# A hybrid attention and state-space block: the last two gate quarters as one pass behind the state-space part

## The chip, the cores and the metric

The kernel runs on one core of a Trainium2 chip. The time is device microseconds for one execution, measured on three runs: 1385.44, 1385.53 and 1386.13 us, median 1385.53. Besides, one execution was recorded by the hardware profiler; its span, from the first to the last instruction, is 1383.8 us, with a mean granted TensorE clock of 0.998.

Names of engines: PE is TensorE (PEld its weight loads), DVE is VectorE, ACT is ScalarE, POOL is GpSimd, SP is SyncE, which here only issues DMAs.

## The reference

256 tokens of width 2048 are normalised and multiplied with one wide matrix `w_in`, whose columns are split into the inputs of an attention branch (q, k, v and a gate z_a), of a state-space branch (z_s, xs, B, C, dt) and two branch gates (g_a, g_s):

```python
hn = rms_norm(x, norm_w)
proj = hn @ w_in
q, k, v, z_a, z_s, xbc, dt_raw, g_a, g_s = jnp.split(proj, split_points, axis=-1)
# attention: 16 heads of 128, three dilated windows, mixed by their log-sum-exp; times silu(z_a)
# state space: causal convolution of 4 taps and silu on xbc, then a chunked scan in 8 groups;
#   y + d_skip * xs, times silu(z_s), rms_norm over 4096
# merge: sigmoid gates g_a, g_s on (o_a @ w_attn_branch) and (y @ w_ssm_branch)
# output: merged @ w_out, plus x, final norm
```

All data is float32. The state-space part has 64 heads of 64 in 8 groups, the chunk is 128 tokens. The quantity that the change is about is g_s, the gate of the state-space branch: four quarters of 512 columns, each x (256 by 2048) times a 2048 by 512 slice of `w_in`, followed by a tanh.

## The kernel before

**Products in parts.** Each float32 operand is split into a high part and a remainder: `unit` loads 128 by 1024 weights (512 KB) through the SP queue into a ring of five, ACT copies the high part h (L276), DVE subtracts it for the remainder l (L277); h and l have four buffers each. A product is then three matmuls, xh·h, xh·l and xl·h (gemm_b L412 to L414; `triple` L476 to L478). Projections of the state-space part and of the heads use pairs, one matmul of 512 columns (L329) and one of 256 (L332).

**Order of the work.** A first block and dt come first, then quarters 0 and 1 of g_s, then the 8 groups of the state-space part. A group projects B, C, four tiles xs and four zs; some steps run later, in the middle of the next group's projections: `turn` transposes xs (tile xtp, L801), `decays` prepares the decay factors gt on ACT (L777 to L791), `scan` multiplies (tile yp, L820), and `gather` (L833 to L838, with the split at L284 and L288) makes from yp, on DVE and ACT, the gated result yT that the branch product reads. Quarter 2 of g_s stands ahead of group 4, quarter 3 behind group 7, each by `gates`. Then come passes over 1024 columns at once, by `gemm_pair`: the state-space branch (ssm, two passes of 16 quads), v (two of 8), later the 16 heads, the gate g_a, the attention branch and the output.

**Quads.** `gemm_pair` takes two k-tiles, two row halves and two column halves of 512 as a quad. A plain quad is 8 products, 24 matmuls. For the quads listed in `S_QUADS` it uses seven products, 21 matmuls (the scheme of Strassen): these need sums and differences of the weights, split into tiles ha/la, hc/lc, htt/ltt and htu/ltu (L543 on ACT, L544 on DVE; L557 makes the difference in wa), and sums of the left operand, the left factors sx_*. A left factor of x or y is computed once (`keep_left`), kept in DRAM and loaded again by `fetch_left`. The differences of the weights can be computed ahead too: `sum_jobs` loads the pieces, does two subtractions on DVE (L252, L253) and spills the result to DRAM, to be loaded as wt when its quad comes. The htt and htu tiles lie in the pool `mul`, which is opened when the pool `ssm` of the state-space part closes, and takes its memory.

**What sets the order.** Python code traces instructions; steps that are due later are put into a list by `after(ticks, f)`, where a tick is one projection or one quad. A scheduler with a timeline model and priorities then fixes each engine's own instruction order. `high_priority` lets the splits of a unit move ahead. On each engine instructions start in that order; between engines, semaphores hold an instruction until what it reads, or the memory it overwrites, is free. `behind_unit(n, f)` runs f when unit n is traced; the small POOL copy at the start of `fetch` and `fetch_left` writes one element of the destination and so holds the load on SP until that unit's h is there.

Of the kernel before, what the change touches and what calls it, by code (L numbers as in the profile page):

```python
# [38 lines left out]
GS_BEFORE = {0: (0, 1), 4: (2,)}  # L39
# [8 lines left out]
    ("ssm", 0): (5, 7, 8, 10, 11, 12, 13), ("ssm", 2): (3, 5, 7, 8, 10, 11, 12, 13),  # L48
    ("v", 0): (2, 3, 4, 5, 6), ("v", 2): (2, 4, 5, 6), ("ga", 0): (2, 4, 5, 6), ("ga", 2): (2, 4, 5, 6),
# [12 lines left out]
SUMS_SSM = [(t, q) for t in (("ssm", 0), ("ssm", 2), ("v", 0), ("v", 2)) for q in S_QUADS[t] if (t[1], q) not in IN_PLACE.get(t[0], ())]  # L62
SUM_UNITS = 2, 9, 16
# [18 lines left out]
def weight_plan():  # L82
# [22 lines left out]
    rows(("gs", 3), "w_in", OFF_GS + 3 * 512, KT)  # L105
# [91 lines left out]
def hybrid_block(ctx: ExitStack, tc: tile.TileContext, wall, xt, x, pk_d, cst_d, fw_d, out):  # L197
# [33 lines left out]

    def behind_unit(n, f):
        on_unit.setdefault(n, []).append(f)
# [4 lines left out]
    def spill(kept, key, name, src, shape):  # L238
        kept[key] = dram.tile([P, *shape], F32, name=name, tag=name)
        nc.sync.dma_start(kept[key], src)  # L240

    def sum_jobs(jobs, units, places):

        def get(tag, q, t, b11, behind):
            n = FIRST[tag] + 2 * q
            for dst, src in ((t, wall[n + 1]), (b11, wall[n, :, :512])):
                gp.tensor_copy(dst[:, 0:1], behind)
                nc.sync.dma_start(dst, src)

        def add(tag, q, t, b11, res, behind):  # L250
            gp.tensor_copy(res[:, 0:1], behind)
            ve.tensor_tensor(res[:, :512], t[:, :512], b11, ALU.subtract)  # L252
            ve.tensor_tensor(res[:, 512:], t[:, 512:], res[:, :512], ALU.subtract)  # L253
            spill(presum, (tag, q), f"t_{tag[0]}{tag[1]}_{q}", res, [UNIT])

        for n, ((tag, q), u) in enumerate(zip(jobs, units)):
            t, b11, res = places[n % len(places)]
            behind_unit(u, lambda behind, a=(tag, q, t, b11): get(*a, behind))
            behind_unit(u + SUM_LAG, lambda behind, a=(tag, q, t, b11, res): add(*a, behind))
# [7 lines left out]
    def unit(n, shape):  # L267
        if n not in loaded:
            load(n)
        w = loaded.pop(n)  # L270
        h = stream.tile([P, UNIT], F32R, name=f"h{n}", tag="h", bufs=H_BUFS)
        l = stream.tile([P, UNIT], F32R, name=f"l{n}", tag="l", bufs=H_BUFS)
        cuts = (0, UNIT // 2, UNIT) if n < N_FINE else (0, UNIT)
        with tc.high_priority(L_AHEAD) if n >= KT // UB else nullcontext():
            for a, b in zip(cuts, cuts[1:]):
                ac.activation(h[:, a:b], w[:, a:b], AF.Copy)  # L276
                ve.tensor_tensor(l[:, a:b], w[:, a:b], h[:, a:b].bitcast(F32), ALU.subtract)  # L277
# [151 lines left out]
    def fetch_left(kept, pool, bufs, key, x, spare, u):  # L429
        def get(behind):  # L430
            sx = new_sx(pool, bufs, spare, f"{key[0]}{key[1]}")
            gp.tensor_copy(sx[:, 0, 0, 0:1], behind)
            nc.sync.dma_start(sx.bitcast(F32), lefts[key])
            kept[key[1]] = left_parts(sx, x, spare)

        behind_unit(u, get)
# [248 lines left out]
    with tc.tile_pool(name="ssm", bufs=2) as sp:  # L685
# [205 lines left out]
        for c in GS_BEFORE[0]:  # L891
# [3 lines left out]
        at = sums_at[:, 3]  # L895
# [3 lines left out]
            [(sums_at[:, 0], sums_at[:, 2, :512], sums_at[:, 1])],  # L899
        )  # L900

        def left_x(q, behind):
            gp.tensor_copy(at[:, 0:1], behind)
            keep_left(("x", q), two_kts(XT, q), 0, at)
# [4 lines left out]
        for g in range(GROUPS):  # L909
# [9 lines left out]
            for t in range(max(4 * g, 1), 4 * g + 4):  # L919
                u, i = divmod(t, 2)  # L920
                acc = project(("xs", t))
                if i == 0:
                    state["xs"].append(new_pair(u, "xs"))
                if t % 4 == 3:
# [3 lines left out]
                    y_lag = Y_LAG + gate  # L928
                    for k in range(4):
# [17 lines left out]
        gates(("gs", 3), th_s, XT)  # L947
# [5 lines left out]
    def scale_gate():  # L953
        tot = bank("m1", 2, "tot_y")
# [21 lines left out]

    with tc.tile_pool(name="xp", bufs=1) as xp:
# [36 lines left out]
    behind_unit(FIRST[("v", 2)] + 1, lambda behind: fetch(dc, cst_d[:, :768], behind))  # L1014
    room = room_of(big.tile([P, 6 * 512], F32, name="room_v", tag="yo0a"), 2, 2)
    with tc.tile_pool(name="vx", bufs=1) as vx:
# [6 lines left out]
        for c in (0, 2):  # L1023
            es, prods = gemm_pair(
                ("v", c), lambda kt: XT[:, kt, :], KT, sx_of_x, c == 2, order=V_ORDERS[c], room=room
# [7 lines left out]
    with tc.tile_pool(name="att", bufs=2) as ap:  # L1033
# [33 lines left out]
        def mix(h, pT, za):  # L1067
# [10 lines left out]
            if h % 2 == 1 and q in ATT_QUADS:  # L1078
# [4 lines left out]
            [  # L1083
                (th_a[:, i, :UNIT], th_a[:, 1, UNIT + 512 * i : UNIT + 512 * i + 512], th_a[:, 0, UNIT:])
                for i in range(2)
            ],
        )

        for h in range(NH):
            q, k = (ap.tile([P, S], F32, name=f"{n}T{h}", tag=f"{n}T", bufs=2) for n in "qk")  # L1090

            for n, d in (("q", q), ("k", k)):
                evac(project((n, h)), d, f"{n}{h}")
# [22 lines left out]
    with tc.tile_pool(name="fin", bufs=2) as fp:  # L1116
# [36 lines left out]
        for n in range(4):  # L1153
# [3 lines left out]
                lambda behind, i=i, cs=cs: fetch(fin[:, i, cs], x[i * P : (i + 1) * P, cs], behind, nc.scalar),  # L1157
# [3 lines left out]
        for n, (tag, u) in enumerate(FW_BEHIND):  # L1161
            cs = slice(n * UNIT, (n + 1) * UNIT)
            behind_unit(
                FIRST[tag] + u, lambda behind, cs=cs: fetch(fw[:, cs], fw_d[cs].partition_broadcast(P), behind, nc.scalar)
# [107 lines left out]
```

## Time and profile before

| | |
|---|---|
| median of three runs | 1385.53 us |
| the profiled execution: span | 1383.8 us |
| PE busy | 1373.6 us, 99% |
| DVE busy | 1169.5 us, 85% |
| ACT busy | 835.5 us, 60% |
| POOL busy | 142.0 us, 10% |
| moved by DMA | 345.00 MB, 249 GB/s on the mean |

Busy times are sums over the whole span. The chain that ended last follows the work back from the last instruction: at each step to what released it, or to the instruction before it on its engine. A row of a group reads: line, engine, operation, out<-in, partitions by elements and type, number, then busy time and mean ns of one, then the idle time of the engine just before and what ended it. A row of the timeline begins with the start in us from the span's start and the duration, and in brackets stands the idle time before it with its releaser. PEq, ACTq, SPq are the sequencers that issue DMAs. A row of PE's waits has the total, the number and the longest. The start of scan 7 is at 580.83 us, the first matmul of the state-space branch at 583.58.

### The profile page before, as it was taken

How to read it: one execution, taken by the hardware profiler on the slowest of the kernel's cores; microseconds unless marked ns; L12 is line 12 of the kernel's file. 1: busy time of each engine (PE TensorE's matmuls, PEld its weight loads, DVE VectorE, ACT ScalarE, POOL GpSimd, SP SyncE). 2: the span in 40 equal slices, each digit the busy share in tenths (PEclk: the TensorE clock that was granted, in tenths of full speed). 3: DMA queues.
4: the chain of work that ended last, by engine and by line, in shares of the span. 5: the costliest groups of instructions: out<-in, count | busy, mean ns of one | idle time of the engine just before them, and what ended most of it. 6: DMA issues, size and time to landing. Idle time of an engine off the chain costs nothing.

```text
span 1383.8 us, 20696 instructions
## 1 busy us (share of the span) xinstructions
PE 1373.6 (99%) x7266; PEld 1169.9 (85%) x7266; DVE 1169.5 (85%) x1753; ACT 835.5 (60%) x1306; POOL 142.0 (10%) x226
## 2 busy tenths in 40 slices
PE   9999999999999999999999999999999999999997
PEld 8888888888888888888888888888888888888886
DVE  7898999987799898789889897777877788888897
ACT  7656677675667675766565554544544556655564
POOL 2301111101011100010001001111111000000112
PEclk9999999999999999999999999999999999999999
DMA  9767988868787866668677668888888757865773
GB/s 347 231 187 225 313 254 291 279 224 287 245 266 240 294 212 208 188 224 280 230 259 267 222 209 278 275 275 273 299 288 301 241 161 264 294 222 180 243 273 122
DMA packets 105080, 345.00 MB, mean 249 GB/s; under 512 B 11728, under 2 KB 13712, under 8 KB 104976
## 3 DMA queue, kind: packets, MB, share of 16 engines
q1 hardware_dynamic: 103536, 339.62, 74.0%
q10 hardware_dynamic: 1440, 4.06, 0.8%
q8 instruction: 57, 0.93, 0.3%
q14 instruction: 47, 0.39, 0.1%
HBM read 314.87 MB, written 28.77 MB: 248 GB/s over the span
## 4 chain that ended last, share of the span: by engine, by line
PE 97%; DMA 1%; DVE 1%; ACT 1%; issue 0%; SPq 0%; POOL 0%; POOLq 0%; DVEq 0%; ACTq 0%
PE ps_zs L329 8%; PE ps_xs L329 8%; PE ps_zs L332 4%; PE ps_q L329 4%; PE ps_za L329 4%; PE ps_k L329 4%; PE ps_xs L332 4%; PE ps_ssm L476 3%; PE ps_ssm L477 3%; PE ps_ssm L478 3%; PE ps_q L332 2%; PE ps_k L332 2%; PE ps_za L332 2%; PE ps_gs L414 2%; PE ps_gs L412 2%; PE ps_gs L413 2%
## 5 line engine op out<-in xcount | busy, mean ns | idle before, releaser
L276 ACT ACTIVATE h<-w 128x1024 fp32r<-128x1024 f32 (+1 forms) x398 | 413.9, 1047 | 318.0 <-issue 78.8
L277 DVE TENSOR_TENSOR l<-w,h 128x1024 fp32r<-128x1024 f32 (+1 forms) x398 | 479.4, 1211 | 124.2 <-ACT h L276 121.8
L329 PE MATMUL ps_zs<-XT,h 128*128 128x512 f32 x496 | 176.3, 397 | 0.0
L329 PE MATMUL ps_xs<-XT,h 128*128 128x512 f32 x496 | 175.9, 396 | 0.0
L332 PE MATMUL ps_zs<-XT,l 128*128 128x256 f32 x496 | 139.9, 282 | 0.0
L332 PE MATMUL ps_xs<-XT,l 128*128 128x256 f32 x496 | 139.8, 282 | 0.0
L329 PEld LDWEIGHTS ps_xs<-XT,h 128*128 128x128 f32 x496 | 93.3, 188 | 21.7
L329 PEld LDWEIGHTS ps_zs<-XT,h 128*128 128x128 f32 x496 | 93.4, 188 | 21.2
L332 PEld LDWEIGHTS ps_zs<-XT,l 128*128 128x128 f32 x496 | 93.7, 189 | 1.5 <-issue 0.7
L332 PEld LDWEIGHTS ps_xs<-XT,l 128*128 128x128 f32 x496 | 93.7, 189 | 0.4
L329 PE MATMUL ps_q<-XT,h 128*128 128x512 f32 x256 | 92.5, 405 | 0.2 <-ACT h L276 0.2
L329 PE MATMUL ps_k<-XT,h 128*128 128x512 f32 x256 | 89.9, 395 | 0.0
L329 PE MATMUL ps_za<-XT,h 128*128 128x512 f32 x256 | 89.7, 394 | 0.0
L543 ACT ACTIVATE ha<-wa 128x1024 fp32r<-128x1024 f32 x43 | 45.4, 1055 | 46.4 <-DMA wa<-in_wall 10.9
L332 PE MATMUL ps_q<-XT,l 128*128 128x256 f32 x256 | 71.2, 278 | 0.0
L332 PE MATMUL ps_k<-XT,l 128*128 128x256 f32 x256 | 71.1, 278 | 0.0
L332 PE MATMUL ps_za<-XT,l 128*128 128x256 f32 x256 | 71.1, 278 | 0.0
L544 DVE TENSOR_TENSOR la<-wa,ha 128x1024 fp32r<-128x1024 f32 x43 | 52.5, 1220 | 11.9 <-ACT ha L543 11.8
L782 ACT ACTIVATE gt<-acb,acT 128x128 f32<-128x128 f32 x128 | 44.2, 391 | 23.7 <-DMA acb<-acum_d 21.9
L329 PEld LDWEIGHTS ps_q<-XT,h 128*128 128x128 f32 x256 | 48.2, 188 | 11.5 <-ACT h L276 0.6
L329 PEld LDWEIGHTS ps_za<-XT,h 128*128 128x128 f32 x256 | 48.1, 188 | 11.3
L329 PEld LDWEIGHTS ps_k<-XT,h 128*128 128x128 f32 x256 | 48.1, 188 | 11.2
(688 smaller groups left out, 3325.1 us busy)
## 6 DMA issues: line engine op xcount, KB each, us to landing
w<-in_wall SPq DMA_DIRECT2D x394, 512.0 KB, 4.7
wa<-in_wall SPq DMA_DIRECT2D x43, 512.0 KB, 4.9
th_a<-in_wall SPq DMA_DIRECT2D x19, 512.0 KB, 5.6
sums_at<-in_wall SPq DMA_DIRECT2D x18, 512.0 KB, 4.7
acb<-acum_d SPq DMA_DIRECT2D x32, 256.0 KB, 4.0
t_ssm<-sums_at SPq DMA_DIRECT2D x13, 512.0 KB, 4.1
wt<-t_ssm SPq DMA_DIRECT2D x13, 512.0 KB, 5.4
th_a<-in_wall SPq DMA_DIRECT2D x19, 256.0 KB, 6.0
```

The lines of the kernel that those rows point to most:

```text
L276: ac.activation(h[:, a:b], w[:, a:b], AF.Copy)
L277: ve.tensor_tensor(l[:, a:b], w[:, a:b], h[:, a:b].bitcast(F32), ALU.subtract)
L329: pe.matmul(acc, h[:, kk, :], m, start=(kt == 0), stop=False)
L332: pe.matmul(acc[:, S:], l[:, kk, :], m[:, :S], start=False, stop=(kt == KT - 1))
L412: pe.matmul(accs[i], xh, h[:, kk], start=(kt == 0), stop=False)
L413: pe.matmul(accs[i], xh, l[:, kk], start=False, stop=False)
L476: pe.matmul(acc, xh, h, start=start, stop=False)
L477: pe.matmul(acc, xh, l, start=False, stop=False)
L478: pe.matmul(acc, xl, h, start=False, stop=stop)
L543: ac.activation(h, src, AF.Copy)
L544: ve.tensor_tensor(l, src, h.bitcast(F32), ALU.subtract)
L782: ac.activation(g4[:, n, b], acb[:, j, b // 2 * P : b // 2 * P + P], AF.Relu, scale=-1.0, bias=sc[:, h : h + 1],)
```

## The change

Quarters 2 and 3 of g_s become one pass of `gemm_pair`, traced behind the state-space part and ahead of the branch passes: eight quads, of which quads 4, 5 and 6 have seven products. Their three left factors are those of x that exist already for v; they are loaded into a pool `gx` at units 5, 6 and 7 of the pass. Their three presums join those made in the state-space part, 24 instead of 18, four in a group, now in place in two pairs of tiles. The decays of the last group are due 1 to 4 ticks after its next-to-last xs tile, and the lag of the scan of group 6 is 7 ticks instead of 11.

The side loads (pieces for presums, left factors, the constants dc, x and the final weights) go from the SP queue, or from ACT behind a POOL copy, to the ACT queue by `side`, whose `issue_after` places the issue behind the latest h split in ACT's order, without a POOL copy. Spills go from SP to POOL's queue. The banks of products and of direct sums are exchanged between the two passes of ssm and of v, and a few small tiles take other banks.

```diff
-GS_BEFORE = {0: (0, 1), 4: (2,)}
+GS_BEFORE = {0: (0, 1)}
+SX_G = (4, 5, 6)
+G_BEHIND = 5, 6, 7
+END_LAG = 7
...
+    ("gs", 2): SX_G,
...
-SUMS_SSM = [(t, q) for t in (("ssm", 0), ("ssm", 2), ("v", 0), ("v", 2)) for q in S_QUADS[t] if (t[1], q) not in IN_PLACE.get(t[0], ())]
-SUM_UNITS = 2, 9, 16
+SUMS_SSM = [(t, q) for t in (("gs", 2), ("ssm", 0), ("ssm", 2), ("v", 0), ("v", 2)) for q in S_QUADS[t] if (t[1], q) not in IN_PLACE.get(t[0], ())]
+SUM_UNITS = 1, 6, 11, 16
...
-    rows(("gs", 3), "w_in", OFF_GS + 3 * 512, KT)
+    pair(("gs", 2), "w_in", OFF_GS + 2 * 512, KT)
...
+    def side(dst, src, queue=nc.scalar):
+        with tc.issue_after(here["high"]):
+            queue.dma_start(dst, src)
...
-        nc.sync.dma_start(kept[key], src)
+        gp.dma_start(kept[key], src)
...
-        def add(tag, q, t, b11, res, behind):
-            gp.tensor_copy(res[:, 0:1], behind)
-            ve.tensor_tensor(res[:, :512], t[:, :512], b11, ALU.subtract)
-            ve.tensor_tensor(res[:, 512:], t[:, 512:], res[:, :512], ALU.subtract)
-            spill(presum, (tag, q), f"t_{tag[0]}{tag[1]}_{q}", res, [UNIT])
+        def add(tag, q, t, b11):
+            with tc.issue_after(here["low"]):
+                ve.tensor_tensor(t[:, :512], t[:, :512], b11, ALU.subtract)
+                ve.tensor_tensor(t[:, 512:], t[:, 512:], t[:, :512], ALU.subtract)
+            spill(presum, (tag, q), f"t_{tag[0]}{tag[1]}_{q}", t, [UNIT])
...
             sx = new_sx(pool, bufs, spare, f"{key[0]}{key[1]}")
-            gp.tensor_copy(sx[:, 0, 0, 0:1], behind)
-            nc.sync.dma_start(sx.bitcast(F32), lefts[key])
+            side(sx.bitcast(F32), lefts[key])
...
+                if t == 4 * GROUPS - 2:
+                    for k in range(4):
+                        after(1 + k, lambda a=(g, k, cb, state): decays(*a))
...
-                    y_lag = Y_LAG + gate
-                    for k in range(4):
+                    y_lag = (END_LAG if g == GROUPS - 2 else Y_LAG) + gate
+                    for k in range(4 if g < GROUPS - 1 else 0):
...
-        gates(("gs", 3), th_s, XT)
         tick(final=True)
...
+    with tc.tile_pool(name="gx", bufs=1) as gx:
+        sx_of_g = {}
+        for n, q in enumerate(SX_G):
+            fetch_left(sx_of_g, gx, len(SX_G), ("x", q), two_kts(XT, q), 0, FIRST[("gs", 2)] + G_BEHIND[n])
+        es, prods = gemm_pair(("gs", 2), lambda kt: XT[:, kt, :], KT, sx_of_g, False)
+        dst = blocks(th_s, 2)
+        fold(prods, dst)
+        for d, e in zip(dst, es):
+            ve.tensor_tensor(d, e, d, ALU.add)
+            ac.activation(d, d, AF.Tanh, scale=0.5)
...
-                ("ssm", c), lambda kt: kt_of(yT, kt), 2 * KT, sxs, c == 2, {} if c else {2: [scale_gate], **{u: [lambda q=q: left_y(q)] for q, u in Y_LATE.items()}},
+                ("ssm", c), lambda kt: kt_of(yT, kt), 2 * KT, sxs, c == 0, {} if c else {2: [scale_gate], **{u: [lambda q=q: left_y(q)] for q, u in Y_LATE.items()}},
```

Scan 7 on PE, before: it stands behind all 96 matmuls of quarter 3 (ps_gs3), directly ahead of the state-space branch (ps_ssm0).

```order
L413 MATMUL ps_gs3_1_6195<-l192_6365,XT_76 128x512
L414 MATMUL ps_gs3_1_6195<-h192_6364,XT_76 128x512
L820 MATMUL yp7_1_6393<-gt7_6196,xdt7_6241 64x256 x2
L820 MATMUL yp7_1_6393<-gt7_6196,xdt7_6241 64x128 x2
...
L820 MATMUL yp7_0_6392<-gt7_6196,xdt7_6241 64x256 x2
L820 MATMUL yp7_0_6392<-gt7_6196,xdt7_6241 64x128 x2
...
L476 MATMUL ps_ssm0_0_6441<-h193_6447,yTa_81 128x512
```

And now: it stands in the gate pass (ps_gs2), behind 73 of its matmuls.

```order
L486 MATMUL ps_gs2_3_6124<-h182_6205,XT_76 128x512
L484 MATMUL ps_gs2_0_6121<-h183_6237,XT_76 128x512
L828 MATMUL yp7_1_6074<-gt7_5860,xdt7_6060 64x256 x2
L828 MATMUL yp7_1_6074<-gt7_5860,xdt7_6060 64x128 x2
...
L828 MATMUL yp7_0_6073<-gt7_5860,xdt7_6060 64x256 x2
L828 MATMUL yp7_0_6073<-gt7_5860,xdt7_6060 64x128 x2
...
L485 MATMUL ps_gs2_0_6121<-l183_6238,XT_76 128x512
```

The scan moved one quad ahead, and 23 plain matmuls of the gate pass now follow it.

PE at the first quad with seven products (quad 4, units 185 and 186; the split tiles of quad 5 are named 187), which begins after those 23:

```order
L486 MATMUL ps_gs2_0_6121<-ha185_6285,XT_76 128x512
L484 MATMUL pp_gs2_0_6275<-ha187_6329,XT_76 128x512
L484 MATMUL ps_gs2_0_6121<-ha187_6329,XT_76 128x512
L485 MATMUL pp_gs2_0_6275<-la187_6330,XT_76 128x512
L486 MATMUL ps_gs2_0_6121<-ha187_6329,XT_76 128x512
L484 MATMUL ps_gs2_2_6123<-htu185_6298,XT_76 128x512
L484 MATMUL ps_gs2_1_6122<-hc185_6289,sx_x4_6209 128x512
L485 MATMUL ps_gs2_1_6122<-lc185_6290,sx_x4_6209 128x512
```

The order holds htu185 as the 36th and the left factor sx_x4 as the 37th matmul behind the scan; before, the first quad with seven products behind the scan came after 96.

ACT at the end of gather 7, before and now. xs15 and yT112 are steps of the gather for the last two tiles; htt, htu and ha are splits for quads with seven products.

```order
L837 ACTIVATE xs15_5968<-y1_15_6420 128x512
L284 ACTIVATE yT112_6135<-y1_15_6420,pk_72 128x256 x2
L543 ACTIVATE htt203_6629<-wt203_6617 128x1024
L284 ACTIVATE yT112_6135<-sxt_y12_6659 128x128
L276 ACTIVATE h199_6571<-w199_6569 128x1024
```

```order
L551 ACTIVATE ha187_6329<-wa187_6323 128x1024
L551 ACTIVATE hc187_6333<-wc187_6326 128x512
L845 ACTIVATE xs15_5846<-y1_15_6101 128x512
L293 ACTIVATE yT112_5738<-y1_15_6101,pk_72 128x256 x2
L551 ACTIVATE htt185_6294<-wt185_6281 128x1024
L551 ACTIVATE htu185_6298<-wa185_6279 128x1024
L551 ACTIVATE ha189_6373<-wa189_6367 128x1024
L240 DMA sx_x4_6209<-sxd_x4_1791 128x1024
L240 DMA sx_x5_6241<-sxd_x5_2199 128x1024
L240 DMA sx_x6_6249<-sxd_x6_2594 128x1024
```

Three splits and then the three loads of left factors now follow the gather on ACT. The gather's DVE part now holds these steps of quad 5 between its own (la187, lc187 and the difference in wa187):

```order
L841 SCALAR_TENSOR_TENSOR y1_15_6101<-xs15_5846,pk_72,yp7_1_6074 128x256 x2
L552 TENSOR_TENSOR la187_6330<-wa187_6323,ha187_6329 128x1024
L844 TENSOR_TENSOR y1_15_6101<-y1_15_6101,zs15_5914 128x512
L552 TENSOR_TENSOR lc187_6334<-wc187_6326,hc187_6333 128x512
L565 TENSOR_TENSOR wa187_6323<-wa187_6323,wt187_6325 128x1024
L846 TENSOR_TENSOR ssq_83<-ssq_83,xs15_5846 128x512
L297 SCALAR_TENSOR_TENSOR yT112_5738<-y1_15_6101,pk_72,yT112_5738 128x256 x2
```

Before, two l subtractions of plain units and a step of a left factor of y (sxt) stood there.

More of the change, by code (lines that the diff above doesn't have):

```diff
@@ L898, in hybrid_block @@
             SUMS_SSM, [FIRST[("B", g)] + n for g in range(1, 7) for n in SUM_UNITS],
-            [(sums_at[:, 0], sums_at[:, 2, :512], sums_at[:, 1])],
+            [(sums_at[:, n], sums_at[:, 3, n * 512 : n * 512 + 512]) for n in range(2)],
         )
         def left_x(q, behind):
-            gp.tensor_copy(at[:, 0:1], behind)
-            keep_left(("x", q), two_kts(XT, q), 0, at)
+            with tc.issue_after(here["low"]):
+                keep_left(("x", q), two_kts(XT, q), 0, at)
         for n, q in enumerate(SX_X + SX_V):
@@ L1156, in hybrid_block @@
                 FIRST[X_BEHIND[n][0]] + X_BEHIND[n][1],
[L1157 removed]
+                lambda behind, i=i, cs=cs: side(fin[:, i, cs], x[i * P : (i + 1) * P, cs]),
             )
```

35 lines of the change are left out of this document (16 added, 19 removed).

## The prediction

> **What bounds the kernel now.** I read the page's busy times first, then the chain that ended last, then the waits of TensorE, and last the stages around the change.
>
> ```profile
> span 1383.8 us, 20696 instructions
> PE 1373.6 (99%) x7266; PEld 1169.9 (85%) x7266; DVE 1169.5 (85%) x1753; ACT 835.5 (60%) x1306; POOL 142.0 (10%) x226
> PE 97%; DMA 1%; DVE 1%; ACT 1%; issue 0%; SPq 0%; POOL 0%; POOLq 0%; DVEq 0%; ACTq 0%
> PE warm L623 <- DVE ssq L620: 1.4, 1, 1.4
> PE ps_first L377 <- ACT h L276: 0.3, 1, 0.3
> PE ps_q L329 <- ACT h L276: 0.2, 1, 0.2
> ```
>
> PE is 97% of the chain, and it waits three times in the whole run, 1.9 us together. So nothing that the change takes off DVE, POOL or the SP queue is worth time by itself. Time comes in three ways: matmuls taken out, a matmul that runs at another pace, and a new wait of PE. The last has no room to hide in: a PE without idle time hands each wait on to the end.
>
> The pace has two readings. The projections of the state-space part are pairs of one 512-column and one 256-column matmul. Two stretches of nothing but such pairs (PE's instruction count, halved, less a few other matmuls: 96 pairs and 64) and two whole groups read so:
>
> ```profile
> 76.80:110.70 33.90, 33.90 (x193) 29.43 (x192) 31.53 (x60) 19.16 (x31) 0.39 (x4) 1.00 0.67 201
> 327.60:349.80 22.20, 22.20 (x130) 19.60 (x129) 17.81 (x28) 12.26 (x19) 2.78 (x6) 1.00 0.82 265
> 172.80:233.10 60.30, 60.30 (x367) 52.38 (x366) 56.45 (x94) 42.48 (x82) 8.91 (x19) 1.00 0.85 274
> 497.40:558.00 60.60, 60.60 (x366) 52.42 (x365) 52.75 (x90) 42.56 (x84) 0.30 (x3) 1.00 0.67 204
> ```
>
> (Columns: the stretch and its length, then busy time of PE, PEld, DVE, ACT, POOL, the granted clock, DMA share, GB/s.) A pair takes 33.9 / 96 = 353.1 ns in the first and 22.2 / 64 = 346.9 ns in the second, at the same granted clock of 1.00, so 6.3 ns a pair depend on something else than the clock. DVE is at 56.45 of 60.3 us in a group: busy, with 3.85 us left.
>
> **The change part by part.**
>
> *Matmuls out.* A plain quad is 24 products of 512 columns, one with seven products 21. Three quads: nine matmuls fewer, which is also the difference of 6869 and 6860 rows on PE. Their pitch is read where the gate quarter ends and the scan follows:
>
> ```profile
> 580.28 0.39 PE L413 MATMUL ps_gs<-l,XT 128*128 128x512 f32 x1
> 580.51 0.39 PE L414 MATMUL ps_gs<-h,XT 128*128 128x512 f32 x1
> 580.83 2.82 PE L820 MATMUL yp<-gt,xdt 128*64 128x256 f32 x32
> 583.58 0.50 PE L476 MATMUL ps_ssm<-h,yTa 128*128 128x512 f32 x1
> 583.92 0.40 PE L477 MATMUL ps_ssm<-l,yTa 128*128 128x512 f32 x1
> 584.15 0.39 PE L478 MATMUL ps_ssm<-h,yTa 128*128 128x512 f32 x1
> ```
>
> Starts lie 0.227 us apart, so −9 × 0.227 = **−2.04 us**.
>
> *The wait at 824.9.* Three of v's second-half presums are now made in the state-space part, so DVE does less ahead of that wait; I count **−0.2 us** (its row above; 0 if it stays).
>
> *The pace.* Reading the starts of the pairs through the state-space part, the faster form begins behind a group's transposes, and the slower one behind its scan or where two h products follow each other. The new order has 17 such places where 8 stood, and the transposes come later; I count about 140 more pairs in the slower form, **+0.9 us** (between −160 pairs, −1.0, and +250, +1.6).
>
> *Presums.* 24 instead of 18 in the state-space part, four in a group instead of three. Each is two subtractions on DVE:
>
> ```profile
> L252 DVE TENSOR_TENSOR sums_at<-sums_at 128x512 f32<-128x512 f32 x18 | 12.4, 690 | 1.0 <-DMA sums_at<-in_wall 0.2
> L253 DVE TENSOR_TENSOR sums_at<-sums_at 128x512 f32<-128x512 f32 x18 | 12.3, 685 | 0.0
> L433 SPq DMA_DIRECT2D sx_x<-sxd_x x5: 326/326/383, 724.7 to 760.5; - x5
> DMA to landing us min/median/max: 3.6/4.9/7.1
> L639 ACTq DMA_DIRECT2D fin<-in_x x4: 335/352/353, 1287.1 to 1335.4; - x4
> ```
>
> 0.69 + 0.69 = 1.38 us more a group: 56.45 becomes 57.8 of 60.3, covered by DVE's idle time; **0**, and up to 6 × 1.38 = 8.3 us where that cover is gone (a rival below). The 105 DMA issues that move to ACT take 0.35 us each there, 37 us over the run, against an ACT that is idle for 40% of it; what POOL and SP lose was covered already. **0** for time on the engines. Where those issues stand in ACT's queue is the next part.
>
> *What the new pass waits for.* This carries the forecast. The gate pass has four plain quads, then quads 4, 5 and 6 with seven products. Scan 7 used to stand behind 96 gate matmuls, now behind 73: "drawn forward" it is by one quad only (its lag stays at 11 ticks; the 7 is for group 6). But what follows it has changed. Before, four plain quads of the state-space branch (96 matmuls) lay between the scan and the first quad with seven products; now it is 23 matmuls. Those quads' operands come out of the split tiles of a pool that sits where the state-space pool closed, and so behind gather 7, which needs scan 7. This cover can be read in the trace of before, from the scan's end at 583.58 on:
>
> ```profile
> 583.70 0.88 DVE L833 SCALAR_TENSOR_TENSOR y<-xs,pk,yp 128x256 f32<-128x256 f32 x2 [0.45 <-PE yp L820]
> 586.00 0.69 DVE L838 TENSOR_TENSOR ssq<-ssq,xs 128x512 f32<-128x512 f32 x1 [0.70 <-ACT xs L837]
> 588.31 1.22 DVE L277 TENSOR_TENSOR l<-w,h 128x1024 fp32r<-128x1024 f32 x1
> 590.50 1.23 DVE L277 TENSOR_TENSOR l<-w,h 128x1024 fp32r<-128x1024 f32 x1 [0.37 <-ACT h L276]
> 592.64 0.68 DVE L448 TENSOR_TENSOR sxt_y<-yT 128x512 f32<-128x512 f32 x1
> 593.24 0.48 DVE L288 SCALAR_TENSOR_TENSOR yT<-y,pk,yT 128x256 fp32r<-128x256 f32 x1
> 593.80 1.06 ACT L543 ACTIVATE htt<-wt 128x1024 fp32r<-128x1024 f32 x1 [2.02 <-DVE yT L288]
> 594.97 1.99 ACT L276 ACTIVATE h<-w 128x1024 fp32r<-128x1024 f32 x2
> ```
>
> The gather ends at 593.24 + 0.48 = 593.72, 10.14 us after the scan, and ACT's first split for a quad with seven products (htt) waits for exactly that and starts 0.08 us later. That cost PE nothing, with 96 × 0.227 = 21.8 us of plain quads ahead.
>
> Now the same chain in the new order, T = 0 at the scan's end. Between the gather's instructions DVE had two l (1.22 + 1.23) and one sxt step (0.68), 3.13 us; it now has la187, lc187 and the wa187 subtraction, by these rows 1.22 + 0.69 + 1.22 = 3.13:
>
> ```profile
> L544 DVE TENSOR_TENSOR la<-wa,ha 128x1024 fp32r<-128x1024 f32 x43 | 52.5, 1220 | 11.9 <-ACT ha L543 11.8
> L544 DVE TENSOR_TENSOR lc<-room_s,hc 128x512 fp32r<-128x512 f32 x13 | 8.9, 686 | 3.5 <-ACT hc L543 3.5
> L557 DVE TENSOR_TENSOR wa<-wa,wt 128x1024 f32<-128x1024 f32 x13 | 15.8, 1219 | 0.0
> ```
>
> So the gather ends at T = 10.1 again. ACT then does htt185 (10.2), htu185 (11.2 to 12.2) and ha189 (from 12.2; the rows above show about 1.0 us from start to start), and only behind them in its queue stand the three loads of the left factors sx_x4, sx_x5 and sx_x6. They need nothing of this: their data has lain in DRAM for long. They are merely queued behind a waiting engine. Issue at 12.1 to 13.2, landing 4.9 us later by the row of these same loads: T = 17.0 to 18.1. PE wants htu185 after 23 + 12 = 35 matmuls, T = 7.9, and sx_x4 after 36, T = 8.2. The wait is 8.9 to 9.9 us; I take **+9.0**, the low end, since weight loads pause when PE does and leave the DMA engines freer. Its bounds: 12.1 + 3.6 − 8.2 = 7.5 and 13.2 + 7.1 − 8.2 = 12.1. Behind it wait PE alone and, through its buffers, the split of later units; nothing is late afterwards, since sx_x5 and sx_x6 land within 1 us of the first.
>
> The Trainium skill, "DMA: Bandwidth & Descriptors", section "Anatomy of one DMA — SWDGE (gpsimd) path", speaks against this place: DMA engines wait for no semaphore, and any wait is held on the issuing sequencer ahead of dispatch. No row of before can test it for ACT, whose ten issues stand where it is free. The same section fits a transfer as 2.0 us + bytes / 436 GB/s; as an estimate a 512 KB left factor would take 3.2 us where the trace has 4.9, and the sum would be 1.7 us less.
>
> *The rest of the pass.* ACT has to split htt189 and h191 in a row before PE reaches h191, nine matmuls (2.0 us) after the buffer comes free: two splits at about 1.0 us each just fit; **+0.3**, between 0 and 1.0. The other moves (swap of banks, presum copies in place, side loads of dc, fin and fw) touch nothing that PE waits for: 0.
>
> *Sum:* −2.04 − 0.2 + 0.9 + 9.0 + 0.3 = **+8.0 us**. The profiled execution has 1383.8 us of span, 1.7 below the median of 1385.53, as before; so span 1391.8, and the time **1393.5 us**. With each term at its bounds: −2.04 − 0.2 − 1.0 + 7.5 + 0 = +4.3 and −2.04 + 0 + 1.6 + 12.1 + 1.0 = +12.7, so 1389.8 to 1398.2 for this case.
>
> **The rivals.** *The loads are in time, the splits are not.* The loads would have to leave by T = 8.2 − 4.9 = 3.3, that is ahead of the gather's ACT work. For it: nothing they need is missing then. Against: ACT's order puts them behind ha189. What stays is htu185, ready at 12.2 against 7.9, +4.3: −1.0 + 4.3 = +3.3, 1388.8.
>
> *No wait at all.* ACT would have to be past ha189 by T = 4.6, and the loads to land in 3.6 us. For it: DVE idles 0.70 + 0.37 us among the gather's rows of before, so the gather can close up a little. Against: its 10.14 us would have to shrink to less than 3. Then −2.04 − 0.2 + 0.9 + 0.3 = −1.0: 1384.5, within what can't be told from no change (0.2%, 2.8 us, is about what a measurement of this kernel tells from nothing: 1382.8 to 1388.3).
>
> *Faster: no wait, and the pace gains.* It ends on the other side where the order that I count as slower turns out faster: place, the state-space pairs; price, 6.3 ns each; with −2.24 from the matmuls and the wait, it decides from 85 pairs (−0.53), and at 160 gives −3.2: 1382.3. For it: gate quarter 2 no longer stands between groups 3 and 4, where the pace changes. Against: it needs the wait to be absent as well.
>
> *DVE runs out in the state-space part, too.* Four presums a group where 1.38 us more go ahead of an l that PE needs. For it: DVE at 57.8 of 60.3. Against: on the average it fits. At half of 8.3, +4.1 on top of the forecast: 1397.6.
>
> **How the numbers follow.** The forecast 0.72, DVE out 0.07, splits alone 0.07, no wait 0.08, faster 0.06. Slower: 0.72 + 0.07 and two thirds of the splits case, 0.83; same: 0.11; faster: 0.06. The range goes from a little below the splits case, 1387.8, to 1399.0, which takes in most of the DVE case; it leaves out the two cases without a wait (0.14) and some 0.05 above.
>
> **What the changed profile would show.** Right: among the waits of PE one at ps_gs near 585 to 600 us, of 7.5 to 12 us in one or two pieces, first for ACT's htu and then for a DMA sx_x<-sxd_x, whose issue stands on ACT's queue behind htt, htu and ha; that htt waits for DVE's yT; a dip of PE in one of the 40 slices near the middle; 9 matmuls fewer, and a state-space part as long as before within 1.6 us. Wrong: no wait of PE above 1 us there, or loads issued ahead of the gather's end; waits of PE for l in the groups would mean the DVE case; a span below 1382 with no wait, the pace.

## The result, and the profile after

The changed kernel takes 1395.76 us (median of four runs, 1394.35 to 1396.4), the kernel before 1385.49 beside it: a ratio of 1.0071, with a 95% interval of 1.0059 to 1.0084. It is slower by 10.3 us; 1393.5 was forecast. The profiled execution has a span of 1393.5 us, 9.7 more than before.

The page of the changed kernel, busy times and chain:

```profile
span 1393.5 us, 20513 instructions
PE 1374.8 (99%) x7257; PEld 1168.7 (84%) x7257; DVE 1181.3 (85%) x1776; ACT 841.6 (60%) x1314; POOL 64.0 (5%) x146
PE 94%; DMA 2%; DVE 1%; ACT 1%; issue 1%; SPq 0%; POOLq 0%; POOL 0%; ACTq 0%; DVEq 0%
```

PE's share of the chain fell from 97 to 94%. Its waits (total, number, longest):

```profile
PE ps_gs L484 <- ACT htu L551: 3.6, 1, 3.6
PE ps_gs L484 <- DMA sx_x<-sxd_x: 1.8, 1, 1.8
PE ps_gs L484 <- ACT h L285: 1.3, 1, 1.3
PE ps_first L386 <- ACT h L285: 1.2, 1, 1.2
PE pp_ga L485 <- DVE ltu L552: 0.5, 1, 0.5
PE pp_ga L484 <- ACT htu L551: 0.2, 1, 0.2
```

Three waits stand in the new gate pass (ps_gs), two in the gate pass of the attention branch (pp_ga), which the change does not mention. From the start of each matmul to that of the next, summed by what it writes, PE spent (us):

| PE time at | before | after | difference |
|---|---|---|---|
| first block and dt | 31.33 | 31.82 | +0.49 |
| state-space groups | 463.19 | 463.84 | +0.65 |
| gs, all four quarters | 87.62 | 95.46 | +7.84 |
| ssm passes | 164.96 | 164.83 | −0.13 |
| v passes | 81.44 | 80.92 | −0.52 |
| heads, attention and output branch | 462.96 | 462.83 | −0.13 |
| ga passes | 82.27 | 83.58 | +1.31 |

The first block is the same in both kernels; in ten other profiles of this study it lies between 30.9 and 32.2, so its 0.49 is not the change's. The gate pass has nine matmuls fewer (−2.04), so +9.88 us were lost in it, and 1.31 in ga.

The chain in the gate pass, PE first: scan 7, the last matmul ahead of the pause, and where PE went on.

```profile
554.89 2.82 PE L828 MATMUL yp<-gt,xdt 128*64 128x256 f32 x32
557.64 0.50 PE L485 MATMUL ps_gs<-l,XT 128*128 128x512 f32 x1
565.48 0.39 PE L486 MATMUL ps_gs<-ha,XT 128*128 128x512 f32 x1
569.51 0.77 PE L484 MATMUL ps_gs<-htu,XT 128*128 128x512 f32 x1 [3.64 <-ACT htu L551]
572.04 0.79 PE L484 MATMUL ps_gs<-hc,sx_x 128*128 128x512 f32 x1 [1.77 <-DMA sx_x<-sxd_x]
572.64 0.63 PE L485 MATMUL ps_gs<-lc,sx_x 128*128 128x512 f32 x1
584.72 0.96 PE L484 MATMUL ps_gs<-h,XT 128*128 128x512 f32 x3 [1.31 <-ACT h L285]
```

And the engines that it waited for, DVE's last step of gather 7, then ACT and its DMA issues:

```profile
566.44 0.88 DVE L297 SCALAR_TENSOR_TENSOR yT<-y,pk,yT 128x256 fp32r<-128x256 f32 x2
567.40 1.06 ACT L551 ACTIVATE htt<-wt 128x1024 fp32r<-128x1024 f32 x1 [1.75 <-issue]
568.37 1.04 ACT L551 ACTIVATE htu<-wa 128x1024 fp32r<-128x1024 f32 x1
568.54 0.82 ACTq L240 DMA_DIRECT2D sx_x<-sxd_x  x2
569.32 1.04 ACT L551 ACTIVATE ha<-wa 128x1024 fp32r<-128x1024 f32 x1
569.38 0.45 ACTq L240 DMA_DIRECT2D sx_x<-sxd_x  x1
```

With T = 0 at 557.64, the gather ends at T = 9.68, htt starts at 9.76, htu ends at 11.77, the first left factor is issued at 10.9 and PE goes on with it at 14.4. PE would have taken htu at 8.07: 3.80 us lost to 569.51, and 2.31 more to 572.04. From there on matmuls start 0.427 us apart instead of 0.227, until 576.05. The table by stretches shows why (columns as in the prediction: the stretch and its length, busy time of PE, PEld, DVE, ACT, POOL, then the granted clock, the DMA share and GB/s):

```profile
565.70:569.50 3.80, 0.17 (x1) 0.03 (x1) 2.63 (x5) 2.10 (x3) 0.00 (x0) 0.99 0.47 138
569.50:572.04 2.54, 0.77 (x1) 0.26 (x1) 2.49 (x3) 0.86 (x1) 0.00 (x0) 0.50 0.94 321
572.04:576.05 4.01, 4.00 (x9) 3.14 (x10) 0.00 (x0) 0.00 (x0) 0.00 (x0) 0.50 0.96 381
576.40:580.00 3.60, 3.60 (x17) 2.98 (x16) 3.21 (x4) 3.14 (x4) 0.00 (x0) 1.00 0.03 7
```

The clock granted to TensorE is 0.50 from the end of the first pause to a little behind 576.05; ten matmuls at that pace cost 2.06 us. A third loss of 1.65 us stands at 584.7. It begins with SP, which issued nothing between wc and the next weights, and ACT's h waited for their landing:

```profile
564.82 0.33 SPq L530 DMA_DIRECT2D wa<-in_wall  x1
570.88 0.33 SPq L534 DMA_DIRECT2D wc<-in_wall  x1
579.17 9.97 SPq L274 DMA_DIRECT2D w<-in_wall  x7
583.61 1.06 ACT L285 ACTIVATE h<-w 128x1024 fp32r<-128x1024 f32 x1 [0.98 <-DMA w<-in_wall]
```

These weights take over the ring buffer from which DVE makes ltt of quad 5, and SP's wait of 7.9 us ahead of them is put down to that ltt. It waited for ACT's htt, and htt for PE, which came late to the split tiles of quad 4:

```profile
576.29 1.06 ACT L551 ACTIVATE htt<-wt 128x1024 fp32r<-128x1024 f32 x1 [5.93 <-PE pp_gs L486]
577.93 1.22 DVE L552 TENSOR_TENSOR ltt<-wt,htt 128x1024 fp32r<-128x1024 f32 x1
```

ltt ends at 579.15 and the load leaves at 579.17. So the third loss follows from the first two.

Together 3.80 + 2.31 + 2.06 + 1.65 = 9.82 of the 9.88 us.

In ga, DVE's last step of a left factor of o and ACT's htu, which takes over the memory from which that left factor is spilled to DRAM; before:

```profile
1130.04 0.69 DVE L286 TENSOR_TENSOR sxt_o<-sxt_o 128x512 fp32r<-128x512 f32 x1
1135.09 1.06 ACT L543 ACTIVATE htu<-wa 128x1024 fp32r<-128x1024 f32 x1 [2.94 <-DMA sxd_o<-sxt_o]
```

and after:

```profile
1138.28 0.69 DVE L295 TENSOR_TENSOR sxt_o<-sxt_o 128x512 fp32r<-128x512 f32 x1
1145.09 1.06 ACT L551 ACTIVATE htu<-wa 128x1024 fp32r<-128x1024 f32 x1 [4.70 <-DMA sxd_o<-sxt_o]
```

From the end of the data to htu it took 4.4 us with the spill on SP, and 6.1 with the spill on POOL. POOL began the issue 0.4 us after the data was there, SP 0.03; the rest is the way to the landing.

### The profile page after: what moved, and what is told of

It is laid out like the page before. It is cut to its first block, busy times and chain, and to the rows that moved or that the text cites. A ratio compares the mean times of both kernels' runs of the same rounds, so it can differ in the third digit from the quotient of the medians.

```text
span 1393.5 us, 20513 instructions
## 1 busy us (share of the span) xinstructions
PE 1374.8 (99%) x7257; PEld 1168.7 (84%) x7257; DVE 1181.3 (85%) x1776; ACT 841.6 (60%) x1314; POOL 64.0 (5%) x146
## 4 chain that ended last, share of the span: by engine, by line
PE 94%; DMA 2%; DVE 1%; ACT 1%; issue 1%; SPq 0%; POOLq 0%; POOL 0%; ACTq 0%; DVEq 0%
PE ps_xs L338 8%; PE ps_zs L338 8%; PE ps_za L338 4%; PE ps_k L338 4%; PE ps_q L338 4%; PE ps_zs L341 4%; PE ps_xs L341 4%; PE ps_ssm L484 3%; PE ps_ssm L485 3%; PE ps_ssm L486 3%; PE ps_q L341 2%; PE ps_k L341 2%; PE ps_za L341 2%; PE ps_out L484 2%; PE ps_out L485 2%; PE ps_out L486 2%
## 5 line engine op out<-in xcount | busy, mean ns | idle before, releaser
L285 ACT ACTIVATE h<-w 128x1024 fp32r<-128x1024 f32 (+1 forms) x392 | 406.9, 1047 | 288.4 <-issue 56.6
L286 DVE TENSOR_TENSOR l<-w,h 128x1024 fp32r<-128x1024 f32 (+1 forms) x392 | 472.6, 1212 | 111.4 <-ACT h L285 106.3
L551 ACT ACTIVATE ha<-wa 128x1024 fp32r<-128x1024 f32 x46 | 48.5, 1055 | 45.7 <-PE ps_ssm L486 10.8
L552 DVE TENSOR_TENSOR la<-wa,ha 128x1024 fp32r<-128x1024 f32 x46 | 56.2, 1222 | 12.8 <-ACT ha L551 10.0
L552 DVE TENSOR_TENSOR ltu<-wa,htu 128x1024 fp32r<-128x1024 f32 x41 | 50.1, 1222 | 13.6 <-ACT htu L551 13.6
L551 ACT ACTIVATE htu<-wa 128x1024 fp32r<-128x1024 f32 x41 | 43.3, 1055 | 28.9 <-DVE wa L565 9.2
```

Source lines behind the costliest of these rows:

```text
L285: here["high"] = ac.activation(h[:, a:b], w[:, a:b], AF.Copy).ins
L286: here["low"] = ve.tensor_tensor(l[:, a:b], w[:, a:b], h[:, a:b].bitcast(F32), ALU.subtract).ins
L551: ac.activation(h, src, AF.Copy)
L552: ve.tensor_tensor(l, src, h.bitcast(F32), ALU.subtract)
```

## The experiments

Theory: the gate pass waits for operands that hang on gather 7, and scan 7 stands too close ahead of it; and ga loses time to spills on POOL's queue. Main rival: the moved loads and the additional presums load ACT, DVE and the DMA engines, and the waits are only where that shows. Times are medians; the kernel before ran at 1385.6 to 1385.7 beside them.

**Spills on SP again.**

```diff
-        gp.dma_start(kept[key], src)
+        nc.sync.dma_start(kept[key], src)
```

> The changed kernel, with the spills (left factors and presums to DRAM) issued from the SP queue again instead of POOL's. Theory: in the ga pass ACT's split htu waited 4.7 us for a spill sxd_o that landed 6.1 us after its data was ready, where it took 4.3 us from SP before; PE lost 1.3 us there. With SP the two waits of PE at pp_ga (0.5 and 0.2 us, with the slower matmuls about them 1.3 us) go: about 1394.5 against 1395.8 of the changed kernel. Rival (the spill holds back weight loads on SP instead): no gain, 1395.8 or more, with a new wait for h.

1391.3 us (1.0040 of before, 1.0027 to 1.0052). PE time in ga is 82.27, that of before to the hundredth, and no wait stands there. The gain of 4.5 us is larger than the 1.3 of that one profile. The profiles explain 2.7 of it: besides ga the state-space groups take 462.98 (−0.86) and gs 94.89 (−0.57, the wait for h is 0.5 us); their first blocks differ by +0.37. The rest of the difference was not traced: the spans profiled are 3.1 us apart, the medians 4.5, and kernels with spills on POOL scatter more (below).

**The kernel before with spills on POOL.** The same edit the other way round.

> The kernel before with one thing of the change: spills are issued from POOL's queue instead of SP's. Theory: the last spill of a left factor of o lands later, and PE gains waits of 1 to 2 us at pp_ga (htu, then ltu), with or without some matmuls at half clock behind them; the state-space part may show short waits for h, too. Above before by 1.3 to 4 us: 1387 to 1389.5. Rival (the loss in ga needs the other moves of the change): as before, 1385.7.

1389.21 us (1.0028, 1.0017 to 1.0039). The one line alone makes the kernel before slower by 3.6 us. In the profile ga takes 83.86 us (+1.59), and ACT's htu waited 4.99 us for the spill. Its seven runs go from 1387.43 to 1391.04, and it is the fastest of them that was profiled; those of the kernel before in that comparison lie within 1384.88 to 1386.98. So this spill lands later from POOL, and not always equally late.

**All quads plain.**

```diff
-SX_G = (4, 5, 6)
+SX_G = ()
...
-        fold(prods, dst)
-        for d, e in zip(dst, es):
-            ve.tensor_tensor(d, e, d, ALU.add)
-            ac.activation(d, d, AF.Tanh, scale=0.5)
+        for d, e in zip(blocks(th_s, 2), es):
+            ac.activation(d, e, AF.Tanh, scale=0.5)
```

> The changed kernel with all eight quads of the gate pass plain: no left factors, no presums and no split tiles for it; all queues, the presums for ssm and v and scan 7 as in the change. Theory: the four losses in the gate pass (waits 3.8 and 2.3, half clock 2.0, h 1.6 us, together 9.7) go, the nine matmuls come back (+2.0): 1395.8 - 9.7 + 2.0 = 1388.1. Rival (the moved queues and presums cost the time, wherever it shows up): the loss of 10 us stays but for the matmuls, 1394 or more.

1389.53 us (1.0026, 1.0016 to 1.0036). No wait is left in the gate pass and gs takes 87.65 us, where the kernel before has 87.62. Only three presums fewer than in the change are made here (21; the gate pass needs none), and all queues are those of the change, so the rival that the moved queues cost the time in the pass falls. What is above the expectation stands in ga (86.51, 2.93 more than in the change, in the profiled run of 1390.73): ACT's htu waited 6.05 us for the spill, PE lost 2.4 us in two pauses, 1.71 and 0.70, and ran at half clock behind them.

**The same with spills on SP.**

> The changed kernel without its seven-product quads (all eight plain) and with spills on SP: what is left of the change is the order (gate pass behind the state-space part, decays, scan of group 6), the loads on ACT's queue, the presums in place and the swap of banks. Theory: with both causes gone no loss remains; the gate pass takes 87.65 us of PE time as before, ga 82.3, and v and the state-space part keep their 0.5 and 0.2 us: 1391.3 - 94.9 + 87.65 = 1384.1, a little below before. Rival (the moved loads cost something that the other losses hid): 1386 or more.

1384.68 us (0.9993, 0.9984 to 1.0002). Without both causes the rest of the change (order, loads on ACT, 21 of the 24 presums, banks) shows no cost, and may gain 0.9 us, which the interval does not tell from zero. gs is 87.65, ga 82.27, v 80.92.

**Tile-wise waits.** The pools of the split tiles and of the left factors wait for the tiles whose memory they take, not for the whole state-space pool. Orders are the same.

```diff
-    mul = ctx.enter_context(tc.tile_pool(name="mul", bufs=1))
+    mul = ctx.enter_context(tc.tile_pool(name="mul", bufs=1, reuse_waits="tile"))
...
-    with tc.tile_pool(name="gx", bufs=1) as gx:
+    with tc.tile_pool(name="gx", bufs=1, reuse_waits="tile") as gx:
```

> The changed kernel; the pools of the split tiles (mul) and of the left factors (gx) wait for the single tiles whose memory they take over, not for the whole state-space pool. Each engine's order is the same; only htt185 loses its wait for the end of gather 7. Theory: htt185 can start when ACT is through with the gather's own split, at 565.7 instead of 567.4, so the first wait of PE (3.6 us by the waits) falls to about 2, the second (sx_x, 1.8) stays, and where the half clock behind them comes from the length of the pause (about 6 us) it may go, too: 1395.8 - 1.7 = 1394.1, or about 1392 without the 2 us at half clock. Rival (the wait for the gather is not what holds htt185): no change, 1395.8.

1398.77 us (1.0095, 1.0081 to 1.0108): slower still, by 3.0 us. The first half came as expected: htt starts right behind ACT's part of the gather and PE's first loss is 1.90 instead of 3.80 us. The second grew to 6.44 us. ACT and its queue in this run, and PE's wait:

```profile
566.01 1.04 ACT L551 ACTIVATE htt<-wt 128x1024 fp32r<-128x1024 f32 x1
566.96 1.04 ACT L551 ACTIVATE htu<-wa 128x1024 fp32r<-128x1024 f32 x1
568.98 1.06 ACT L551 ACTIVATE ha<-wa 128x1024 fp32r<-128x1024 f32 x1 [0.98 <-DMA wa<-in_wall]
569.00 1.30 ACTq L240 DMA_DIRECT2D sx_x<-sxd_x  x3
PE ps_gs L484 <- DMA sx_x<-sxd_x: 6.2, 1, 6.2
```

Now ha189, ahead of the loads in the queue, waited for a weight load, and all three left factors went out behind it, at 569.00 although ACT was free from 568.0. Counted from the scan's end that is T = 10.9, the same as in the changed kernel: the earlier splits gained the loads nothing. So the wait for the pool's release is a cause of the first loss, and the place behind other waits on ACT's queue is a second cause, which the first had covered. What made the run slower than the change is something else. The loads took 5.7 us to PE's matmul, against 3.5 in the changed kernel; SP's load of wt189 left 0.07 us ahead of them here (568.93) and 1.2 us behind them there (569.75), but that this is the reason was not tested. gs is 96.83 (+1.37), and ga 85.25 (+1.67), for POOL's spill.

**Left factors from SP.** With tile-wise waits and spills on SP, the loads are traced with units 0 to 2 of the pass and issued by SP, where they stand behind the load of wa189 and not behind its split.

```diff
-G_BEHIND = 5, 6, 7
+G_BEHIND = 0, 1, 2
...
-            side(sx.bitcast(F32), lefts[key])
+            if pool.name == "gx":
+                nc.sync.dma_start(sx.bitcast(F32), lefts[key])
+            else:
+                side(sx.bitcast(F32), lefts[key])
```

> The changed kernel with spills on SP and tile-wise waits; and the three left factors of the gate pass are loaded from SP's queue, where they stand behind the load of wa189 and not behind ACT's split of it. Theory: SP issues them at about 565.2 instead of 568.5 us, so sx_x4 lands at 569 to 570; the wait for htu is 1.9 us as in the run with tile-wise waits, and the wait for sx_x4 0.5 to 2 us in place of 2.4 to 6.4. If the half clock behind the waits needs a pause of more than about 4 us, it goes, too: 1391.3 - 2.5 to 4 - 2 = 1385.5 to 1387, and 1387.5 to 1389 if it stays. Rival (a left factor lands late because the DMA engines are full, whatever queue it is on): the wait stays at 5 us or more, 1391 or more.

1389.41 us (1.0025, 1.0016 to 1.0035), 1.9 less than with spills on SP alone. Issue of the loads, and two stretches further on:

```profile
563.74 1.64 SPq L442 DMA_DIRECT2D sx_x<-sxd_x  x3
578.80:581.10 2.30, 0.24 (x2) 0.00 (x0) 0.71 (x1) 1.04 (x2) 0.00 (x0) 1.00 0.84 289
581.50:584.90 3.40, 3.40 (x9) 2.65 (x8) 2.57 (x3) 2.93 (x4) 0.00 (x0) 0.50 0.72 245
```

The two losses fell to 1.90 and 1.88 us, so the queue does decide when the left factors come. But the half clock stayed, for 3.0 us behind these two, and the wait for h grew to 2.30 us, with another 3.4 us at half clock behind it. The weights for that h did not come later: counted from the scan's end SP issued them at 18.4 us (21.5 in the change), as soon as DVE's ltt of quad 5 was done, and PE went on with them at 25.0 (27.1). But PE had lost less on the way and wanted them at 22.7 (25.6), and they took 5.5 us from SP's issue to ACT's h, against 4.4. In the profiled run, the slowest of ten (1391.34; the fastest took 1387.8), the gate pass as a whole (95.04) gained nothing over 94.89. The median is just above what was expected for the case that the half clock stays; the growth of the third wait was not expected.

**Two quads with seven products** (5 and 6), spills on SP.

```diff
-SX_G = (4, 5, 6)
-G_BEHIND = 5, 6, 7
+SX_G = (5, 6)
+G_BEHIND = 6, 7
```

> The changed kernel with spills on SP (1391.3 in the run of that change alone), and two quads with seven products (5 and 6) in place of three, so that 59 gate matmuls (13.4 us) lie between the scan and htu187 and 60 ahead of sx_x5, in place of 35 and 36. Theory: the operands need a fixed time from the scan's end, about 12 us for htu and 15 to 17.5 for the left factor, so htu comes in time and the wait for sx_x5 is 1.5 to 4 us; of the 9 us lost in the pass 2 to 5 remain, three matmuls come back (+0.7): 1391.3 - 9.0 + 0.7 + 2 to 5 = 1385 to 1388. Rival (the seven-product quads as such are too dense for ACT and DVE): waits as long as with three, 1391.

1383.54 us (0.9983, 0.9974 to 0.9992). PE loses 0.27 us in the pass, less than expected, and that at an h, not at htu or a left factor. The cover came out longer than counted: in this run's order 64 matmuls (14.6 us) lie between the scan and htu187, and not 59. The left factor was issued 11.2 us after the scan's end and used, without a pause, at 14.9. So the operands need at most 14.9 us here, as they needed 14.4 in the change, where the landing of 4.9 us led to 15 to 17.5.

**The last group's xs tiles first.** The four zs projections then lie between the last xs tile and the gate pass, so that scan 7 comes 20 gate matmuls into the pass, and 82 matmuls lie between it and htu185.

```diff
+def tiles_of(g):
+    ts = range(max(4 * g, 1), 4 * g + 4)
+    if g == GROUPS - 1:
+        return [("xs", t) for t in ts] + [("zs", t) for t in ts]
+    return [(name, t) for t in ts for name in ("xs", "zs")]
...
-                        after(1 + k, lambda a=(g, k, cb, state): decays(*a))
+                        after(3 + k, lambda a=(g, k, cb, state): decays(*a))
```

> The changed kernel; in the last group the four xs tiles are projected ahead of the four zs tiles, and its decays come two ticks later, so that scan 7 stands 20 matmuls into the gate pass instead of 73, and 82 matmuls (18.6 us) lie between it and htu185. Theory: the operands need some 17 to 18 us from the scan's end (gather 10, splits 2 to 3, load 5), so the waits at ps_gs vanish or stay under 1 us: 1395.8 - 9.7 = 1386.1. Rival (another limit holds the seven-product quads, such as ACT or the weight loads in the pass): waits of 3 us or more remain there, 1390 or more.

1387.31 us (1.0012, 1.0003 to 1.0021). The waits for htu and sx_x are gone with all three quads and all queues of the change: gs takes 86.37 us, 9.1 less than in the change; a wait for h that costs 0.65 us remains in the pass. The rest of the distance to 1386.1 are ga (84.26) and two waits for h in the groups (1.8 us), with spills still on POOL.

**Both together:** xs tiles first and spills on SP.

> The changed kernel with the last group's xs tiles first and spills on SP. Theory: the two causes add up: the gate pass as in the run with xs first alone (86.4 us of PE time where the change has 95.5), ga as before the change (82.3): 1391.3 - 94.9 + 86.4 = 1382.8, below the kernel before. Rival (the short waits for h in the state-space part, 1.8 us in the run with xs first, come from the new order and not from POOL's spills): 1384.5.

1382.53 us (0.9978, 0.9969 to 0.9988): faster than the kernel before by 0.2% (3.0 us) and than the change by 13.2 us. The page, the scan, the issue of the left factors and their use:

```profile
span 1380.2 us, 20472 instructions
541.28 2.82 PE L834 MATMUL yp<-gt,xdt 128*64 128x256 f32 x32
558.41 1.30 ACTq L246 DMA_DIRECT2D sx_x<-sxd_x  x3
562.98 0.39 PE L490 MATMUL ps_gs<-hc,sx_x 128*128 128x512 f32 x1
```

gs takes 85.83 and ga 82.27, and the waits for h in the groups are gone as well. Only the queue of the spills differs between the two runs, so those waits, too, are put down to POOL, by one profile of each; a single loss of up to 0.5 us stands in the groups of other runs with spills on SP. The left factors are issued 14.4 us after the scan's end (544.03) and used 4.57 us later, without a pause.

**A fourth quad with seven products** (3) ahead of the three in that kernel.

```diff
-SX_G = (4, 5, 6)
-G_BEHIND = 5, 6, 7
+SX_G = (3, 4, 5, 6)
+G_BEHIND = 4, 4, 5, 5
```

> The fastest kernel so far (xs first, spills on SP, 1382.5) with a fourth quad with seven products, quad 3, ahead of the three. In that kernel ACT issued the left factors 14.4 us after the scan's end, and PE wanted the first one at 19.0, 4.6 us after its issue. With quad 3 it wants it 21 to 24 matmuls earlier, some 5 us. Theory: a wait of 3 to 5 us for sx_x (with or without 2 us at half clock behind it), three matmuls less (-0.7): 1382.5 - 0.7 + 3 to 7 = 1385 to 1389. Rival (the gather and the loads move up with their user): 1381.8.

1386.79 us (1.0007, 0.9999 to 1.0016), 4.3 above the kernel with three. PE loses 0.88 us to htu and 1.14 us to the left factor, and some 2 us more to later operands of the pass:

```profile
557.56 1.30 ACTq L246 DMA_DIRECT2D sx_x<-sxd_x  x3
PE ps_gs L490 <- DMA sx_x<-sxd_x: 0.9, 1, 0.9
```

The cover between scan and first quad with seven products is again too short (htu was used at 15.5 us and the left factor at 16.9, where PE would have gone on at 14.6), and three matmuls fewer (0.7 us) do not pay for it.

## Why the prediction was right

*Matmuls out*, −2.04: right; gs with its pauses taken off is at that count.

*The wait at 824.9*, −0.2: it went, and the v passes lost 0.52 us of PE time. Right in kind, 0.3 too small.

*The pace*, +0.9: wrong. All projection matmuls of the state-space part together take 429.11 us before and 429.15 after. In the other kernels of the new order with spills on SP they take 428.3 to 429.1. The term should have been 0 or a little below; that order sets the pace at such places was read from two stretches and did not carry over to a count of places.

*Presums and issues on ACT*, 0: right. No wait for l appears in the groups of the changed profile, DVE's rows have 24 presums at 0.69 us a half, and the fastest kernel of this study makes all 24. *DVE runs out* falls with this.

*Spills on POOL* stood among the moves that were put at nothing ("what POOL and SP lose was covered already"). That step failed: the kernel before loses 3.6 us by it alone. What was lost was not POOL's time but the time to the landing, and ga's htu stands behind that landing: 4.4 to 4.6 us behind the data in the seven profiles with spills on SP, 6.1 to 7.8 in the five with POOL; the trace of before showed the wait already (ACT 2.94 us for sxd_o), with PE just not reached by it.

*What the new pass waits for*, +9.0: the mechanism is what happened, link by link, from gather to htt, htu, left factor. Its times were 9.68 for the gather's end (forecast 10.1), 11.77 for htu's (12.2), 10.9 for the issue (12.1 to 13.2) and 14.4 for the landing (17.0 to 18.1). So the wait itself was 6.1 us, 2.9 less than said: the landing was taken at the median of 4.9 us where it took 3.5, and the issue was set behind ha189, while it left 0.8 us before ha189 started. The sentence "nothing is late afterwards" failed the other way, by the 2.06 us at half clock and 1.65 us for the weights of the next plain unit. The pass lost 9.82 us where 9.0 + 0.3 were forecast; that the sums agree so well is luck in part: two errors cancelled. The cover of the kernel before, which the change had to give up, was somewhat shorter than the 96 matmuls and 21.8 us that were counted for it: on PE, where the matmuls of several quads stand mixed, the first operand of a quad with seven products was used behind 84 matmuls, at T = 18.3 (601.89). It was enough all the same. The Trainium skill's rule, "DMA: Bandwidth & Descriptors", section "Anatomy of one DMA — SWDGE (gpsimd) path", that any wait is held on the issuing sequencer, agrees with the run with tile-wise waits, where three loads stood behind a split that waited for its weights. Its fit is for DMAs issued from POOL; the estimate of 3.2 us that it gives for 512 KB is near the 3.5 us measured here from ACT's queue, where PE stood and SP issued only two loads meanwhile. In the two runs with tile-wise waits it was 5.7 from ACT's queue and 4.5 from SP's.

*The rest of the pass*, +0.3 for h191 behind htt189: such a wait is there, with 1.65 us, but its cause is a late weight load on SP and not the two splits on ACT. SP held that load for 7.9 us until DVE's ltt of quad 5 was done, which hung on PE's own pauses; in the three other runs with these pauses the load left within 0.05 us of the same ltt. Without the pauses the wait shrinks, to 0.65 us (xs tiles first), 0.27 (two such quads) and none (the fastest kernel).

*Rivals.* That the loads are in time and the splits not, that nothing waits, and that the pace gains: none came. That the change does less than its words say is so for the last scan, which moved by one quad only; with the group's xs tiles first it moves by 53 matmuls more, and the loss in the pass is gone.

## What to carry to other kernels

A unit of work that is drawn forward shortens the cover of everything that hangs on its neighbours: count the matmuls between the producer (here the scan) and the first consumer of whatever is released behind it, before and after. Here the left factor was there 14.4 to 16.9 us after the scan in the runs where PE waited for it from ACT's queue, the change left 8, and with covers of 14.6 and 18.7 us two and three such quads gained.

A load that needs nothing is still held by the waits ahead of it in its queue, and a spill that nobody reads soon still holds the memory it is read from. When DMAs change queues, look up who waits for their landing, not whether the queue is free.

## What the hardware showed unexpectedly

TensorE's granted clock falls to 0.50 behind pauses that are short, and the length of a pause alone does not decide it. In the traces here the changes of the granted clock lie multiples of 3.41 us apart: the half rate lasted 6.83 us in the change, 10.24 with tile-wise waits alone, 3.41 behind the two pauses in ga with all quads plain, and twice 3.41 with left factors from SP, where 10.24 lay between the two. Counted back from a change in such stretches, those at full rate in which PE stood idle (by starts of its matmuls more than 0.227 us apart) for 2.08 us or more (2.08, 2.30, 2.68 and above) were followed by half rate, and those with 1.66 us or less were not. So 2.30 us alone was enough, and 1.71 and 0.70 us close together, while 2.02 us in ga with tile-wise waits was not: it fell on two stretches, 1.66 and 0.36. The clock was back at 1.00 some 3.0 to 4.6 us after PE went on. The Trainium skill, "TensorE: Matmul & The Clock Gate", section "🔬 Part 1: The HAM clock gate (the "warmup" mystery)", puts it down to an idle window of about 3.4 us; the half rate, the length of the stretches and the time until it is back agree with the rows here, while 2.08 us of idle time in a stretch was enough. Price here: 1.5 to 2.3 us of slower matmuls for each fall.

A DMA issue on ACT's queue left 0.78 us before the activation ahead of it started (568.54 against 569.32): here the queue held a load behind another instruction's wait (569.00 with tile-wise waits), not behind its run.

The last 512 KB spill of a left factor of o landed later from POOL's queue than from SP's in every profile, and its time scatters more (6.1 to 7.8 us against 4.4 to 4.6 from the data to htu); with one edited line the runs of the kernel before spread over 3.6 instead of 2.1 us. It does not hold for each spill: with that line the median from issue to landing grew in eight of nine groups (t_ga from 5.4 to 6.9) and fell in one (sxd_x from 5.2 to 4.2).
